# Moving weight splits and the turning of the next rows inside the expert stage of a decoder layer

## The chip, the cores and the metric

The kernel runs on one core of a Trainium2 chip. The metric is the device time of one execution in microseconds (us); lower is better. A core has five engines that run side by side, each through its own instructions in order: TensorE (PE in the profile; its weight loads are PEld), VectorE (DVE), ScalarE (ACT), GpSimd (POOL) and SyncE (SP). They wait for one another by semaphores. Here SyncE issues the plain DMAs and GpSimd the indirect ones, which gather or scatter rows by an index.

## The reference

The layer is a mixer (sliding-window attention beside an mLSTM), a cross attention and a mixture of experts, for 2048 tokens of width 1024, in float32. The change touches only the experts:

```python
def hierarchical_moe(xn, ...):          # 32 experts, top 2 within the best of 4 groups
    ...
    x_pad = zeros.at[dest].set(xt[token_idx[order]])   # tokens sorted by expert, in blocks
    def expert_block(args):
        xb, e = args
        hb = jax.nn.silu(xb @ w_g[e]) * (xb @ w_u[e])  # 1024 -> 512
        return hb @ w_d[e]                             # 512 -> 1024
    y_pad = lax.map(expert_block, ...)
    y = y_pad[dest] * gates[order][:, None]
    out = zeros.at[token_idx[order]].add(y)
```

After that the layer's sum is normalised (`norm_final`). How many tokens an expert has depends on the data: 128 on average, more for some and fewer for others.

## The kernel before

Products are made in float32 precision from two float32r halves, hi and lo: `split` makes hi on ScalarE (a cast) and lo on VectorE (the difference), and three matmuls (hi by hi, hi by lo, lo by hi) give one product (`mm3`, L125 to L127). Weights are split too. One expert has 12 weight pieces of 128 x 1024: four of the gate (w_g), four of up (w_u), four of down (w_d). They are loaded by SyncE into a ring of 9 raw tiles (`we_raw`) and split into a ring of 16 places (`we_hi`, `we_lo`); a raw tile's next load is issued when its split is done (`next_load`). So an expert's 12 pieces and four of the next one's are held at once, and the split of piece 4 of the next expert writes the place of piece 0 (gate) of this one.

The loop over the 32 experts (`phase3`) handles each in these steps, and expert x works ahead for x+1 and x+2:

- the full block A of 128 rows: gate product, SiLU (`full_gate`, run for x+1 at the end of x), up product, product with the gate weight (`times`), turning of the hidden rows by TensorE (`turn_h`), turning of the next expert's A rows (`next_rows(x, 0)`), and the gather of the A rows of x+2 on GpSimd;
- a branch on the count. With more than 128 tokens, `half_within` does a block B of 64 rows: its gate and up products, SiLU, turning of the hidden rows and down product, and a scatter-add of the result to DRAM. Here hi and lo of the 64 rows lie side by side in one operand of 128 columns, so the two halves of the sums come out on different partitions and are added (`both`: a ScalarE copy and a VectorE add). Of the 8 splits that are due, four (`todo[:4]`, up pieces of x+1) are done in this arm: `step(1)` behind SiLU, `step(3)` behind the down product. Without block B, the other arm does these four splits alone. With more than 192 tokens, `later_blocks` handles further blocks L of 64 rows; since the four splits have overwritten the gate pieces, these are first loaded again (`reload`), through the tiles `again` and `yA`;
- the down product of A (`full_down`, `down_turn`), with the other four splits (`todo[4:]`) and, behind its third quarter (k == 2), the turning of the next expert's B rows (`next_rows(x, 1)`: eight transposes, then a cast and a subtraction in `put`) and the gather of the B rows of x+2.

As built, the first two quarters of A's down product (12 matmuls `pu<-..hT`) stand ahead of the branch on TensorE; the order on TensorE, ScalarE and VectorE is as the code is written inside `as_written` (a chain of order-only dependencies). From expert 10 or so on, finished rows are also normalised and given out in between (`norm`): squares on ScalarE, the root on GpSimd, scaling on VectorE.

Tiles: `both` holds the B rows of the next expert in its upper 64 partitions (`xg["B"]`) and block B's hidden rows and results in its lower 64 (`hu`); `xTB` is the turned form of B rows, `xTA` of A rows; `hTB` the turned hidden rows of block B; `pt`, `pu`, `pd`, `pg` are PSUM tiles, three for `pt`; `yA` is the sum of A before its scatter-add. A block L's rows go to `yA` and their turned form to `xTB`.

Of the kernel before, what the change touches and what calls it, by code (L numbers as in the profile page):

```python
# [10 lines left out]
F32R = mybir.dt.float32r  # L11
# [8 lines left out]
P = 128  # L20
# [11 lines left out]
HB = 64  # L32
# [11 lines left out]
def together(*parts):  # L44

    parts = [iter(p) for p in parts]
    while parts:
        parts = [p for p in parts if next(p, p) is not p]


def by(n, part):

    for i, _ in enumerate(part):
        if i % n == n - 1:
            yield
# [11 lines left out]
class Net:  # L67
# [1338 lines left out]
    def phase3(self):  # L1406
        nc, tc, a = self.nc, self.tc, self.a
        with ExitStack() as cx:
            e = lambda **k: cx.enter_context(tc.tile_pool(reuse_waits="tile", **k))
            self.io = e(name="io3", bufs=1)  # L1410
            self.sm = e(name="sm3", bufs=2)
            self.we2 = e(name="we2", bufs=1)
            self.ps_g = e(name="ps_g", bufs=1, space=PSUM)
            self.ps_u = e(name="ps_u", bufs=2, space=PSUM)
            self.ps_t = e(name="ps_t3", bufs=3, space=PSUM)
            self.ps_d = e(name="ps_d", bufs=2, space=PSUM)
            t = lambda name, shape, dt=F32: self.io.tile(shape, dt, name=name)


            both = t("both", [P, D])  # L1420
            self.xg, self.hu = {"A": t("xgA", [P, D], F32R), "B": both[HB:P, :]}, both[:HB, :]
            self.hT = [t(f"hT{i}", [P, 4, P], F32R) for i in range(2)]
            self.xT = {tg: [t(f"xT{tg}{i}", [P, 8, P], F32R) for i in range(n)] for tg, n in (("A", 2), ("B", 1))}

            self.yA = t("yA", [P, D])

            self.again = t("again", [P, D])
            self.xg["L"], self.xT["L"] = self.yA[:HB, :], self.xT["B"]
            for g in self.xg.values():
                nc.vector.memset(g.bitcast(F32), 0.0)  # L1430

            self.flags = t("flags", [1, 2, NEXP], I32)
            for i, n in enumerate((P, P + HB)):
                nc.vector.tensor_scalar(out=self.flags[:, i, :], in0=self.counts[:, :NEXP], scalar1=float(n), scalar2=None,
                                        op0=ALU.is_gt)
            self.infos = [self.expert_info(x) for x in range(3)]
            rows = [self.expert_rows(0, b) for b in range(2)]
            with self.as_written():
                self.weights_ahead(9)
                self.turned_rows(*rows[0])()  # L1440
                self.weights_ahead(10)
                self.turned_rows(*rows[1])()
                self.weights_ahead(12)
                for b in range(2):
                    self.expert_rows(1, b)
                cnt, flags = self.full_gate(0, self.ws)
            self.open_norm()
            for x in range(NEXP):
                ws, self.ws = self.ws[:12], self.ws[12:]
                if x + 3 < NEXP:  # L1450
                    self.infos.append(self.expert_info(x + 3))
                todo = self.next_splits(8)
                last = x + 1 == NEXP
                if last:
                    self.late_norms()
                norm = self.norm_ahead(x)
                with self.as_written():
                    self.full_up(x, ws)
                with tc.If(cnt > P, label=f"more{x}") as more:  # L1459
                    self.hint(f"most{x}", flags)  # L1460
                    self.group_puts = []
                    with self.as_written():
                        ahead = norm() if last else None
                        self.half_within(x, ws, todo[:4], ahead)
                        if last:
                            self.full_down(x, ws, [], ahead)
                    self.later_blocks(x, cnt, ws, todo[:4])
                with more.Else():
                    self.group_puts = []
                    with self.as_written():  # L1470
                        if last:
                            self.full_down(x, ws, [], norm())
                        else:
                            self.splitter(todo[:4])(4)
                if not last:
                    with self.as_written():
                        self.full_down(x, ws, todo[4:], norm())
                        cnt, flags = self.full_gate(x + 1, self.ws)
# [211 lines left out]
    def half_within(self, x, ws, todo, norm):  # L1690

        info, step = self.infos[x][1], self.splitter(todo)
        h, u, hT = self.half_tiles()
        pg = self.pd()
        self.gate(pg, "B", ws)
        pu = [self.half_pu(0)]
        self.up(pu[0], "B", ws, 0)
        self.half_silu(h, pg)
        step(1)
        self.half_times(h, u, pu[0], info, 0)  # L1700
        pu.append(self.half_pu(1))
        self.up(pu[1], "B", ws, 1)
        self.turn_h(h, hT, 0)
        self.half_times(h, u, pu[1], info, 1)
        pd = [self.pd() for _ in range(2)]
        self.down(pd, hT, ws, (0,))
        self.turn_h(h, hT, 1)
        self.down(pd, hT, ws, range(1, 4))
        step(3)
        self.half_out(self.hu, pd, info, "B", norm)  # L1710

    def later_blocks(self, x, cnt, ws, over):
# [25 lines left out]
    def down_turn(self, pd, hT, x, ws, step, norm, late):  # L1738
        for k in range(4):
            self.down(pd, hT, ws, (k,))  # L1740
            step(2 if k == 1 else 1)
            if k == 2:
                self.next_rows(x, 1)()
            self.steps(norm, k == 2, late[k])
        info = self.infos[x][0]
        y = self.sums_of.get("A", self.yA)
        for n in range(2):
            yn = y[:, n * 512:n * 512 + 512]
            if self.sums_of:
                self.nc.vector.tensor_tensor(out=yn, in0=pd[n], in1=yn, op=ALU.add)  # L1750
            else:
                self.nc.scalar.copy(out=yn, in_=pd[n])  # L1752
        if self.sums_of:
            out = [(info, self.yA), *self.due]
            self.due = []
            ssq, r = self.stats(P, len(out))
            self.square(y, ssq, 0)
            self.gain(self.nc.vector, y, self.yA)
            root = self.root_steps(ssq, r)
            next(root)  # L1760
            next(root)
            for at, y in out[1:]:
                self.gain(self.nc.vector, y)
            together(by(2, root), norm)
            for j, (at, y) in enumerate(out):
                rj = r[:y.shape[0], j:j + 1]
                if j:
                    self.nc.scalar.activation(out=y, in_=y, func=AF.Copy, scale=rj)
                else:
                    self.nc.vector.tensor_scalar(out=y, in0=y, scalar1=rj, scalar2=None, op0=ALU.mult)  # L1770
                self.give_apart(at, y)
        else:
            self.add_rows(info, y)
# [265 lines left out]
```

## Time and profile before

| | |
|---|---|
| median of 3 runs | 2336.86 us (2336.54 to 2350.87) |
| the profiled execution | 2337.82 us |
| its span, first to last instruction | 2336.1 us |
| granted TensorE clock over the span | 0.95 |
| TensorE busy | 2091.7 us (90%) |
| VectorE busy | 1558.4 us (67%) |
| ScalarE busy | 1272.3 us (54%) |
| GpSimd busy | 445.1 us (19%) |
| DMA, mean | 186 GB/s |

The busy times are of one profiled execution, from whose own time a sum is to be made. A row's busy share is a mean over stages with different limits; what a step is worth is read in its stage, from what ends a wait last. [...]

### The profile page before, as it was taken

The page shows a single profiled execution, that of the slowest core. Times are in us where ns is not written, and L with a number is a line of the kernel's source. Part 1 is how long each engine was busy: PE and PEld are TensorE (multiplying, and loading weights), DVE is VectorE, ACT ScalarE, POOL GpSimd, SP SyncE. Part 2 cuts the span into 40 slices and gives each one's busy share as a digit, 9 for nine tenths or more (in the row PEclk, how much of TensorE's full clock was granted, in tenths as well). Part 3 has the DMA queues.
Part 4 walks back from the last instruction along what each step waited for, and adds up shares of the span by engine and source line. Part 5 has one row for each costly group of instructions (what it writes and reads, how often), then busy time and mean ns, then how long its engine had stood idle before and what let it go on. Part 6 is the DMA issues. An engine that isn't in the chain of part 4 may idle for free. (4 is left out here: it accounts for less than half of the span.)

```text
span 2336.1 us, 36449 instructions
## 1 busy us (share of the span) xinstructions
PE 2091.7 (90%) x12173; PEld 1790.3 (77%) x12173; DVE 1558.4 (67%) x3586; ACT 1272.3 (54%) x2479; POOL 445.1 (19%) x536
## 2 busy tenths in 40 slices
PE   6999999999999999899985695799999898988985
PEld 5998888988878888898974573677877777777764
DVE  6278876478776756577767453775877768776665
ACT  6267875368763332444542442654766657666553
POOL 1000000000000000133323110111222433523325
PEclk9999999999999999999998797899999999899997
DMA  5533444534578876334555662876988879987743
GB/s 167 127 113 105 116 140 135 133 101 114 145 190 232 231 199 182 118 127 101 114 148 101 188 220 90 269 269 213 315 271 275 282 236 320 314 310 259 248 135 92
DMA packets 266262, 434.75 MB, mean 186 GB/s; under 512 B 53232, under 2 KB 175216, under 8 KB 265952
## 3 DMA queue, kind: packets, MB, share of 16 engines
q1 hardware_dynamic: 245216, 381.25, 52.9%
q0 software_dynamic: 20736, 49.85, 8.1%
q8 instruction: 135, 2.21, 0.4%
q14 instruction: 175, 1.43, 0.2%
HBM read 356.97 MB, written 92.71 MB: 192 GB/s over the span
## 5 line engine op out<-in xcount | busy, mean ns | idle before, releaser
L77 DVE TENSOR_TENSOR we_lo<-we_raw,we_hi 128x1024 fp32r<-128x1024 f32 x384 | 449.1, 1220 | 118.4 <-ACT we_hi L76 111.8
L76 ACT CAST we_hi<-we_raw 128x1024 fp32r<-128x1024 f32 x384 | 380.8, 1054 | 50.6 <-SPq L1459 20.1
L125 PE MATMUL pu<-we_hi,xTA 128*128 128x256 f32 x512 | 148.8, 291 | 25.2 <-ACT yA L1752 25.2
L125 PE MATMUL mm<-hT,w_hi 128*128 128x512 f32 x416 | 166.4, 401 | 0.9 <-ACT hT L327 0.9
L126 PE MATMUL mm<-hT,w_hi 128*128 128x512 f32 x416 | 166.1, 399 | 0.0
L127 PE MATMUL mm<-hT,w_lo 128*128 128x512 f32 x416 | 165.9, 399 | 0.0
L127 PE MATMUL mm<-w_hi,hT 128*128 128x324 f32 (+1 forms) x512 | 152.6, 298 | 0.0
L125 PE MATMUL mm<-w_hi,hT 128*128 128x324 f32 (+1 forms) x512 | 152.6, 298 | 0.0
L126 PE MATMUL mm<-w_lo,hT 128*128 128x324 f32 (+1 forms) x512 | 152.0, 297 | 0.0
L126 PE MATMUL pu<-we_lo,xTA 128*128 128x256 f32 x512 | 148.0, 289 | 0.0
L127 PE MATMUL pu<-we_hi,xTA 128*128 128x256 f32 x512 | 147.7, 288 | 0.0
L125 PE MATMUL pu<-we_hi,hT 128*128 128x512 f32 x256 | 113.0, 441 | 18.6 <-PEq L1459 7.4
L589 POOL TENSOR_TENSOR sq<-sq 128x256 f32<-128x256 f32 x16 | 12.6, 786 | 589.6 <-ACT sq L586 589.6
L125 PEld LDWEIGHTS pu<-we_hi,xTA 128*128 128x128 f32 x512 | 100.5, 196 | 30.1 <-ACT yA L1752 29.1
L126 PE MATMUL pu<-we_lo,hT 128*128 128x512 f32 x256 | 107.1, 418 | 0.0
L127 PE MATMUL pu<-we_hi,hT 128*128 128x512 f32 x256 | 105.1, 411 | 0.0
L125 PE MATMUL pg<-we_hi,xTA 128*128 128x512 f32 x256 | 103.8, 406 | 0.0
L126 PE MATMUL pg<-we_lo,xTA 128*128 128x512 f32 x256 | 103.4, 404 | 0.0
L127 PE MATMUL pg<-we_hi,xTA 128*128 128x512 f32 x256 | 102.5, 400 | 0.0
L126 PEld LDWEIGHTS pu<-we_lo,xTA 128*128 128x128 f32 x512 | 100.4, 196 | 0.9
L127 PEld LDWEIGHTS pu<-we_hi,xTA 128*128 128x128 f32 x512 | 100.5, 196 | 0.0
L125 PEld LDWEIGHTS mm<-w_hi,hT 128*128 128x128 f32 x512 | 96.5, 188 | 1.4 <-ACT o_ev L484 0.8
(501 smaller groups left out, 6067.5 us busy)
## 6 DMA issues: line engine op xcount, KB each, us to landing
we_raw<-in_w_e_gate_dram SPq DMA_DIRECT2D x128, 512.0 KB, 7.3
we_raw<-in_w_e_up_dram SPq DMA_DIRECT2D x128, 512.0 KB, 6.6
we_raw<-in_w_e_down_dram SPq DMA_DIRECT2D x128, 512.0 KB, 9.5
w_raw<-in_w_in_dram SPq DMA_DIRECT2D x56, 256.0 KB, 3.6
q_in<-q_d SPq DMA_DIRECT2D x32, 256.0 KB, 4.3
qk_d<-acc SPq DMA_DIRECT2D x32, 256.0 KB, 3.4
at_d<-at SPq DMA_DIRECT2D x32, 256.0 KB, 2.9
at_in<-at_d SPq DMA_DIRECT2D x32, 256.0 KB, 7.6
```

Of the source, the lines that this page charges most:

```text
L76: first = nc.scalar.copy(out=hi, in_=src)
L77: (low or nc.vector).tensor_tensor(out=lo, in0=src, in1=hi.bitcast(F32), op=ALU.subtract)
L125: first = mm(ps, lhsT=wh, rhs=xh, start=start, stop=False)
L126: mm(ps, lhsT=wh, rhs=xl, start=False, stop=False)
L127: mm(ps, lhsT=wl, rhs=xh, start=False, stop=stop)
L589: nc.gpsimd.tensor_tensor(out=sq[:, 0:2], in0=sq[:, 0:2], in1=sq[:, 2:4], op=ALU.add)
```

## The change

In `half_within`, two of the four splits move ahead of SiLU (`step(2)` right behind the gate product), the other two stay behind the down product (`step(2)` for `step(3)`). The turning of the next B rows, with the gather that follows it, leaves `down_turn` and goes into both arms: in `half_within` its transposes stand behind the turning of B's first hidden half and its cast and subtraction behind those of the second; in the other arm the transposes stand ahead of the four splits and the cast and subtraction behind them. Since `xTB` then already holds the next expert's rows when `later_blocks` runs, a block L's rows get a turned form of their own (`xTL`, 4 KB more in each partition) and are gathered into `hu`.

```diff
@@ phase3
-            self.xg["L"], self.xT["L"] = self.yA[:HB, :], self.xT["B"]
+            self.xg["L"], self.xT["L"] = self.hu, [t("xTL", [P, 8, P], F32R)]
...
                         else:
+                            put = self.next_rows(x, 1)
                             self.splitter(todo[:4])(4)
+                            put()
@@ half_within
         self.gate(pg, "B", ws)
+        step(2)
         pu = [self.half_pu(0)]
         self.up(pu[0], "B", ws, 0)
         self.half_silu(h, pg)
-        step(1)
         self.half_times(h, u, pu[0], info, 0)
         pu.append(self.half_pu(1))
         self.up(pu[1], "B", ws, 1)
         self.turn_h(h, hT, 0)
+        put = self.next_rows(x, 1)
         self.half_times(h, u, pu[1], info, 1)
         pd = [self.pd() for _ in range(2)]
         self.down(pd, hT, ws, (0,))
         self.turn_h(h, hT, 1)
+        put()
         self.down(pd, hT, ws, range(1, 4))
-        step(3)
+        step(2)
         self.half_out(self.hu, pd, info, "B", norm)
@@ down_turn
             step(2 if k == 1 else 1)
-            if k == 2:
-                self.next_rows(x, 1)()
             self.steps(norm, k == 2, late[k])
```

Line numbers in rows of the changed kernel are 3 higher in these functions (L1617 is L1620, L1620 is L1623, L1795 is L1798, L1800 is L1803, L1779 is L1782, L1582 is L1585).

On ScalarE, in the arm with block B, before: behind the branch come the copy of the gate sums and SiLU (L1795, L1800), the first weight cast, the copies of the two up products with the cast of the turned hidden half between them, and three weight casts.

```order
L1459 COMPARE_AND_BRANCH
L1795 COPY both<-pd 64x512
L1800 ACTIVATE both<-both 64x512
L76 CAST we_hi_14564<-we_raw_13928 128x1024
L1795 COPY both<-pd 64x256
L76 CAST hTB<-pt_19921 128x2x64
L1795 COPY both<-pt_19904 64x256
L76 CAST hTB<-pt_19935 128x2x64
L76 CAST we_hi_14569<-we_raw_13930 128x1024
L76 CAST we_hi_14576<-we_raw_8236 128x1024
L76 CAST we_hi_14581<-we_raw_8237 128x1024
```

The same place on ScalarE now.

```order
L1460 COMPARE_AND_BRANCH
L76 CAST we_hi_14565<-we_raw_13928 128x1024
L76 CAST we_hi_14570<-we_raw_13930 128x1024
L1798 COPY both<-pd 64x512
L1803 ACTIVATE both<-both 64x512
L1798 COPY both<-pd 64x256
L76 CAST hTB<-pt_20051 128x2x64
L1798 COPY both<-pt_20034 64x256
L76 CAST hTB<-pt_20077 128x2x64
L76 CAST xTB_14423<-pt_20056 128x8x64
L76 CAST we_hi_14577<-we_raw_8236 128x1024
L76 CAST we_hi_14582<-we_raw_8237 128x1024
```

Two weight casts moved ahead of the first copy, none stands between SiLU and the copy of the up product, and the cast of the next B rows (`xTB`) came in behind the second hidden half.

On TensorE, in the same arm, before: the last up matmul, the first two transposes of the hidden rows (L1779), the first quarter of B's down product, the next two transposes.

```order
L1617 MATMUL pt_19904<-we_hi_9304,xTB_14423 128x256
L1779 MATMUL pt_19921<-ident,both 128x64 x2
L1617 MATMUL pd<-we_hi_14454,hTB 128x512
L1620 MATMUL pd<-we_lo_14455,hTB 64x512
L1617 MATMUL pd<-we_hi_14454,hTB 128x512
L1620 MATMUL pd<-we_lo_14455,hTB 64x512
L1779 MATMUL pt_19935<-ident,both 128x64 x2
```

The same place on TensorE now.

```order
L1620 MATMUL pt_20034<-we_hi_9304,xTB_14423 128x256
L1782 MATMUL pt_20051<-ident,both 128x64 x2
L120 MATMUL pt_20056<-ident,both 128x64 x8
L1620 MATMUL pd<-we_hi_14455,hTB 128x512
L1623 MATMUL pd<-we_lo_14456,hTB 64x512
L1620 MATMUL pd<-we_hi_14455,hTB 128x512
L1623 MATMUL pd<-we_lo_14456,hTB 64x512
L1782 MATMUL pt_20077<-ident,both 128x64 x2
```

The eight transposes of the next B rows (L120, source `both`) came in between the hidden rows' first transposes and the down product.

On TensorE, in A's down product behind the join of the arms, before: the second half of its third quarter, the eight transposes, the start of the last quarter.

```order
L125 MATMUL pu<-we_hi_14464,hT_14419 128x512
L126 MATMUL pu<-we_lo_14465,hT_14419 128x512
L127 MATMUL pu<-we_hi_14464,hT_14420 128x512
L120 MATMUL pt_20272<-ident,both 128x64 x8
L125 MATMUL pu<-we_hi_14469,hT_14419 128x512
```

The end of the arm without block B on TensorE now, the join (L1460) and the start of the third quarter.

```order
L120 MATMUL pt_20369<-ident,both 128x64 x8
L1460 UNCONDITIONAL_BRANCH
L125 MATMUL pu<-we_hi_14465,hT_14419 128x512
L126 MATMUL pu<-we_lo_14466,hT_14419 128x512
L127 MATMUL pu<-we_hi_14465,hT_14420 128x512
```

The transposes moved out of the product to the head of the join; that arm held no TensorE work before.

## Rows read from the trace of the kernel before

**Rows 1.** Busy us (instructions) by stretch, clock, DMA share, GB/s: experts 0, 8; sum.

```profile
1304.60:1342.20 37.60, 33.78 (x185) 27.74 (x185) 23.48 (x31) 21.56 (x31) 5.54 (x4) 0.95 0.65 215
...
1606.70:1642.60 35.90, 32.08 (x186) 26.47 (x184) 21.78 (x29) 19.39 (x30) 6.29 (x5) 1.00 0.65 207
...
sum 520.90, PE 470.22 PEld 382.54 DVE 325.46 ACT 288.09 POOL 120.37; mean PE 33.59 PEld 27.32 DVE 23.25 ACT 20.58 POOL 8.60
```

**Rows 2.** The same view for expert 5, without block B.

```profile
1513.60:1533.80 20.20, 20.05 (x117) 17.17 (x116) 16.87 (x19) 14.69 (x20) 4.55 (x4) 1.00 1.00 351
```

**Rows 3.** Order of time in block B of expert 7: start, us, what, [idle before <-releaser].

```profile
1586.18 0.39 PE L1617 MATMUL pd<-we_hi,xTB 128*128 128x512 f32 x1
...
1590.05 0.58 ACT L1795 COPY both<-pd 64x512 f32<-64x512 f32 x1 [4.87 <-PE pd L1617]
...
1590.67 0.68 DVE L1796 TENSOR_TENSOR both<-pd,both 64x512 f32<-64x512 f32 x1 [4.66 <-ACT both L1795]
...
1591.38 0.63 ACT L1800 ACTIVATE both<-both 64x512 f32<-64x512 f32 x1 [0.75 <-DVE both L1796]
...
1591.60 0.29 PE L1617 MATMUL pd<-we_hi,xTB 128*128 128x256 f32 x1
...
1591.92 1.03 ACT L76 CAST we_hi<-we_raw 128x1024 fp32r<-128x1024 f32 x1
...
1592.86 0.36 ACT L1795 COPY both<-pd 64x256 f32<-64x256 f32 x1
...
1592.98 1.23 DVE L77 TENSOR_TENSOR we_lo<-we_raw,we_hi 128x1024 fp32r<-128x1024 f32 x1 [1.63 <-ACT we_hi L76]
...
1594.13 0.41 DVE L1796 TENSOR_TENSOR both<-pd,both 64x256 f32<-64x256 f32 x1
1594.57 0.48 DVE L1641 SCALAR_TENSOR_TENSOR both<-both,infoA 64x256 f32<-64x256 f32 x1
...
1595.20 0.31 PE L1779 MATMUL pt<-ident,both 64*128 64x64 f32 x2 [1.45 <-DVE both L1641]
...
1596.18 0.50 PE L1617 MATMUL pd<-we_hi,hTB 128*128 128x512 f32 x1 [0.68 <-DVE hTB L77]
```

**Rows 4.** TensorE's waits in the expert stage: waiter, releaser: us, times, longest.

```profile
PE pt L1779 <- DVE both L1641: 21.7, 15, 1.5
PE pt L120 <- DMA yA<-xn_d,infoB: 21.2, 1, 21.2
PE pd L1617 <- DVE hTB L77: 12.3, 17, 1.4
...
PE pt L120 <- DVEq L1714: 7.0, 6, 1.3
```

**Rows 5.** Order of time on TensorE in A's down product of expert 28.

```profile
2200.13 1.14 PE L120 MATMUL pt<-ident,both 64*128 64x64 f32 x8 [1.29 <-DVEq L1714]
```

**Rows 6.** Busy us by stretch, as rows 1, inside expert 7.

```profile
1597.25:1600.66 3.41, 3.41 (x10) 2.32 (x10) 1.87 (x3) 2.82 (x4) 0.00 (x0) 0.50 0.03 7
```

**Rows 7.** SyncE's queue in order of time, ahead of expert 7's block B.

```profile
1573.35 1.48 SPq L1513 DMA_DIRECT2D we_raw<-in_w_e_up_dram  x3
```

**Rows 8.** DMA issues of the page: count, KB each, us to landing.

```profile
we_raw<-in_w_e_up_dram SPq DMA_DIRECT2D x128, 512.0 KB, 6.6
```

**Rows 9.** Order of time on ScalarE, the copies of expert 22's sums.

```profile
2022.10 1.07 ACT L1752 COPY yA<-pu 128x512 f32<-128x512 f32 x2 [3.66 <-DMA out_dram<-y_fin,list]
```

**Rows 10.** Order of time in expert 2, from the last reload to block L's gate.

```profile
1430.47 1.23 DVE L77 TENSOR_TENSOR we_lo<-yA,we_hi 128x1024 fp32r<-128x1024 f32 x1 [1.62 <-ACT we_hi L76]
1431.97 0.96 POOL L1582 DMA_INDIRECT yA<-xn_d,infoB  x1 [14.96 <-DVE we_lo L77]
...
1434.98 1.19 PE L120 MATMUL pt<-ident,yA 64*128 64x64 f32 x8 [21.23 <-DMA yA<-xn_d,infoB]
...
1444.36 0.58 ACT L1795 COPY both<-pd 64x512 f32<-64x512 f32 x1 [7.56 <-PE pd L1617]
```

**Rows 11.** TensorE's branches at the arms: count, ns min/median/max, first and last start.

```profile
L1459 PEldq COMPARE_BRANCH  x32: 70/218/6019, 1318.4 to 2289.8; - x32
```

## The prediction

> **What bounds the kernel now.** I read the granted clock and busy times by stretch first, then the order of time inside one expert, then who waited for whom. The change touches the expert stage alone, which runs from 1304.6 us to the end at 2336.1 us. Call the expert at place x of the loop "expert x". The 16 experts with more than 128 tokens also run a 64-row block B; 14 of them (all but 2 and 31) take 520.9 us, 37.2 us each, with TensorE marked busy for 33.6 us and a clock of 0.95 in most [rows 1]. An expert without block B takes 20.2 us of which TensorE is busy 20.05, at clock 1.00 [rows 2]. So where there is no block B, TensorE is the limit and has no hole; where there is one, the block costs 17 us, and the holes must lie in it.
>
> The order of time in expert 7 shows them [rows 3]. TensorE starts B's gate product at 1586.18. ScalarE, idle for 4.87 us, copies the upper half of the gate sums at 1590.05; VectorE adds (0.68), ScalarE does SiLU (0.63, ended at 1592.0). Then the queue order bites: ScalarE next casts a weight tile (1.03), so the copy of the first up product starts only at 1592.86 although that product was done at 1591.9; and VectorE's 1.23 us subtraction for the same split sits ahead of the add (1594.13) and the product with the gate weight (1594.57). TensorE, through with the second up product at 1593.75, gets its input at 1595.17: a hole of 1.45 us. A second hole, 0.68 us, follows, since the down product needs both halves of the turned tile just made. The chain of waits has these as 21.7 us in 15 and 12.3 us in 17 places [rows 4]. A third one: the eight transposes of the next B rows inside the full block's down product wait 1.29 us in expert 28 for VectorE's last work of the arm [rows 5], 7.0 us in 6 places altogether [rows 4]. And after such holes the clock halves: 0.50 for 3.41 us in expert 7 [rows 6].
>
> **The change part by part.** All sums are against the profiled execution, 2337.82 us (span 2336.1 and 1.7 around it); the median of the runs shown is 1.0 us below that.
>
> *Two splits ahead of SiLU.* Nothing is added: 2 casts and 2 subtractions move from behind SiLU into ScalarE's 4.87 us of idle time. They write the ring places of the gate weights that block B is just reading, so the first must wait until B's gate has used its first piece, which is 4 of 16 matmuls at 0.23 us, 1.1 us after its start (1586.18 becomes zero). Casts: 1.1 to 2.1 and 2.1 to 3.1. Subtractions: 2.1 to 3.4 and 3.4 to 4.6. The copy of the gate sums comes at 3.9 as before and ends at 4.45; the add can start at 4.6 instead of 4.5 and ends at 5.3; SiLU ends at 5.9; the copy of the first up product ends at 6.3, its add at 6.7, the product at 7.2. TensorE ends the second up product at 7.6. The hole of 1.45 us closes with 0.4 us to spare: 14 times 1.42 is 19.9 us. The cover is the gate product's 3.8 us; without it each split would push SiLU by 1.2 us. The weight tiles to be split are there: the later of the two loads was issued at 1573.35, 12.8 us ahead, and a load of this kind lands after 6.6 us in the median [rows 7, 8]; among the 16 block-B experts that lead is 11 us at the shortest. SyncE then issues the two refilling loads up to 8 us earlier, which costs nothing and helps.
>
> *The next 64 rows turned inside the arm.* The eight transposes (1.14 us in [rows 5]) leave the full block's down product and stand behind the first transposes of B's own hidden tile. There they fill the 0.68 us hole and the rest is the time they took anyway: 14 times 0.68 is 9.5 us. With them out of the down product, the 7.0 us of waits for the end of VectorE's arm go. The cast (0.59) and subtraction (0.68) of the turned rows stand behind those of B's second hidden half, before the two remaining splits, where only the arm's closing copies follow. In the other arm (16 experts) the same eight transposes come 1.4 us earlier on TensorE, and cast and subtraction come before four splits instead of after: TensorE's count is unchanged, and those splits feed the next expert's down product, some 15 us on. I cost it at nothing; it would cost up to 1.3 us an expert if ScalarE and VectorE had no slack there. On GpSimd the gather of the rows after next is issued in the arm, ahead of the scatter-add of B, whose data is ready only at the arm's end. In the other arm it comes ahead of the queue's pass through the join, for which ScalarE's copies of the sums (yA) wait where GpSimd runs late, as at 2022.10 [rows 9]; one gather more in that path, and one less since the A gather now precedes the root steps: between -0.7 and +0.7 us in 6 experts, taken as 0, bounds 4 us either way.
>
> *The clock.* The 14 experts lose (1 - clock) x length, worked out over the 14 rows and summed, 22.0 us. Expert 8 has the same first two holes and 1.00 [rows 1], so holes do not always cost it; an expert without holes has 1.00 [rows 2]. If 1.42, 0.68 and 1.29 go, what is left is 0.4 us at the arm's end. I take 20.0 of the 22.0 as won; the bounds are 0 and 22.0.
>
> *Rows of the late block.* One expert (2) has more than 192 tokens. Its third block gathered its rows into yA, which is also a reload tile, so the gather waited for the last reload's subtraction: 1430.47 plus 1.23, gather at 1431.97, transposes at 1434.98 and a gate product that ended at 1444.33 [rows 10], after 21.2 us without work for TensorE [rows 4]. With a tile of its own the rows are turned while the four reloads run, and the gate ends one piece (4 matmuls, at half clock 1.7 us) after the last subtraction at 1431.7, near 1433.5: 10.8 us less. TensorE stays at half clock a little longer, up to 1.7 us; I take 9, bounds 7 and 12. Expert 2's block B wins 4 us like the others.
>
> Sum: 19.9 + 9.5 + 7.0 + 20.0 + 9 + 4 = 69.4 us; 2337.8 - 69.4 = 2268.4. Expert 31 has no weights left to split and no next rows: nothing. **Forecast: 2268 us.** What is next late in the arm is VectorE, which ends its last add some 3 us after TensorE's last B matmul; nothing of TensorE waits for that once the transposes are gone.
>
> **Rivals.** *The clock is not won back.* The holes shrink but the arm's end still has 0.4 us and a branch; with 0 of 22.0 the time is about 2290. For it: some holes fell without a halving and others with it, so the link isn't one to one. Against it: the holeless experts at 1.00.
>
> *The splits are held to the end of the gate product* (so the change does not do what it says). If the release of the weights' places comes only with the gate's last matmul, both casts start at 3.9, the second subtraction ends at 7.3, add 8.0, SiLU 8.6, copy 9.0, product 9.95, where today it ends at 8.9: the first hole grows by 1.0 us, 14 us in all, no clock is won, 9.5, 7.0 and 9 stay: 2337.8 - 11.5, near 2326, no change. Against it: ScalarE's copy at 1590.05 was released in the middle of TensorE's stream, by one matmul of it [rows 3]. [...]
>
> *Branch fetch, the slower side.* Of TensorE's 32 branches at the start of the arms one took 6.02 us, with a median of 0.22 [rows 11]. The arm without block B held no TensorE work and now does, and the way from one arm to the join gets longer. If 16 entries and 16 exits each took half of that longest one, 3.0 us, that is 96 us against 69: 2364. It decides from 23 more such holds on. Against it: the added code is eight transposes and a jump an expert, and half of the branches took 0.22 us or less. [...]
>
> **How the numbers follow.** Forecast 0.72; clock not won 0.13 (2290); splits held 0.07 (2326); branch fetch 0.03 (2364); more than I count, below 2252, 0.05. The range takes in the first two with their bounds: all of the clock, 12 for the late block and 4 from GpSimd give about 2259 and some more for shorter stalls elsewhere 2252; no clock, 7 for the late block and 4 lost to GpSimd give 2296, with a few us for the spread of runs 2300. The measurement tells about 1% (the runs shown spread by 0.6%): faster by over 1% is below 2313.5, so faster 0.90, same 0.07, slower 0.03.
>
> **What would show it.** In the profile after: ScalarE's two casts inside B's gate product and none between SiLU and the next copy; TensorE's wait before B's first transposes gone from the list of waits, or down to a few tenths; no wait at the transposes of the next rows in either arm; the 14 block-B experts at 32 to 34 us with clock 1.00; the late gather issued before the reloads end. The forecast is wrong if the casts start after the gate's last matmul, if the half clock stays in these experts, if TensorE in the other arm waits for rows not yet gathered, or if experts without block B grow beyond 20.2.

## The result and the profile after

The changed kernel takes 2265.45 us in the median of 6 runs (2258.9 to 2277.3), the kernel before 2341.16 in 6 (2336.5 to 2350.9): a ratio of 0.969, interval 0.967 to 0.971. The profiled executions are 2258.90 against 2337.82 us, 78.9 less, with spans of 2257.2 and 2336.1.

First the expert stage by stretches (us from and to, length, busy us of each engine with its count of instructions, granted clock, DMA share, GB/s): the first of the 14 experts with block B, expert 7, and the sum of the 14.

```profile
1301.00:1334.40 33.40, 32.96 (x185) 27.48 (x185) 21.43 (x30) 19.54 (x28) 3.61 (x4) 0.96 0.72 254
...
1540.20:1572.20 32.00, 31.56 (x186) 26.32 (x185) 22.00 (x29) 18.95 (x29) 5.12 (x5) 1.00 0.71 234
...
sum 471.20, PE 447.67 PEld 372.03 DVE 326.07 ACT 285.06 POOL 131.02; mean PE 31.98 PEld 26.57 DVE 23.29 ACT 20.36 POOL 9.36
```

The 14 took 520.9 us before [rows 1] and take 471.2, 49.7 less. Expert 7 takes 32.0 us at a clock of 1.00. It took 36.1 at 0.95 in the profile before:

```profile
1570.60:1606.70 36.10, 33.53 (x186) 27.33 (x185) 21.88 (x29) 18.27 (x28) 5.46 (x5) 0.95 0.66 208
```

The records of the granted clock, a share of full speed, read 1.00 or 0.50 in both profiles and nothing between, so 0.95 is a mean over time at each. In expert 7 before, TensorE's 128x512 matmuls started 0.43 us apart inside the stretch at 0.50 [rows 6] and 0.23 behind it, so that four took 1.7 us at half clock, as the prediction has it for the late block:

```profile
1599.07 0.63 PE L1617 MATMUL pd<-we_hi,hTB 128*128 128x512 f32 x1
1599.50 0.63 PE L1620 MATMUL pd<-we_lo,hTB 128*64 128x512 f32 x1
1599.92 0.63 PE L1617 MATMUL pd<-we_hi,hTB 128*128 128x512 f32 x1
...
1600.73 0.39 PE L1617 MATMUL pd<-we_hi,hTB 128*128 128x512 f32 x1
1600.96 0.40 PE L1620 MATMUL pd<-we_lo,hTB 128*64 128x512 f32 x1
1601.19 0.39 PE L1617 MATMUL pd<-we_hi,hTB 128*128 128x512 f32 x1
```

In the same view expert 5, without block B, and the sum of the 16 without block B, after the change:

```profile
1488.50:1508.30 19.80, 19.80 (x118) 17.29 (x117) 17.36 (x20) 15.11 (x22) 4.54 (x3) 1.00 1.04 367
...
sum 357.70, PE 326.99 PEld 284.93 DVE 285.22 ACT 249.18 POOL 144.17; mean PE 20.44 PEld 17.81 DVE 17.83 ACT 15.57 POOL 9.01
```

Expert 5 had 20.2 us [rows 2]. The sum of the 16 in the profile before:

```profile
sum 372.80, PE 336.26 PEld 286.44 DVE 293.23 ACT 251.37 POOL 132.62; mean PE 21.02 PEld 17.90 DVE 18.33 ACT 15.71 POOL 8.29
```

So the 16 lost 15.1. Expert 2 (with the late block) went from 79.4 to 68.2, expert 31 from 58.4 to 59.0, and the stage began 3.5 us earlier. 49.7 + 15.1 + 11.2 - 0.6 + 3.5 is 78.9: the whole difference.

TensorE's waits in the expert stage (waiter, releaser: us, times, longest), against [rows 4]:

```profile
PE pu L125 <- ACT yA L1755: 32.9, 7, 11.8
PE pt L120 <- DMA both<-xn_d,infoB: 17.0, 1, 17.0
PE pt L1782 <- DVE hA L1644: 8.5, 8, 3.2
PE pu L126 <- PEq L1719: 5.2, 8, 2.1
PE pt L120 <- DVE we_lo L77: 3.1, 2, 1.8
PE pd L1620 <- DVE hTB L77: 2.0, 2, 1.4
```

The group of 21.7 us at B's first transposes is gone, that of 12.3 us at B's down product is down to 2.0 in experts 2 and 31, and the 7.0 us for the end of VectorE's arm are gone. At the top, as before the change, stands the wait for yA, now 32.9 us. Waits for TensorE's own branch at the start of the arms (L1459), 7.4 us before, are no longer in the list. The two lines before:

```profile
PE pu L125 <- ACT yA L1752: 25.2, 7, 11.0
PE pu L125 <- PEq L1459: 7.4, 4, 3.0
```

Block B of expert 7 in order of time on ScalarE, VectorE and TensorE (start, us, what, [idle before <- releaser]), to be read against [rows 3]; the gate product starts at 1555.84.

```profile
1556.97 2.00 ACT L76 CAST we_hi<-we_raw 128x1024 fp32r<-128x1024 f32 x2 [2.14 <-PE pd L1620]
1559.73 0.58 ACT L1798 COPY both<-pd 64x512 f32<-64x512 f32 x1 [0.76 <-PE pd L1620]
1561.07 0.64 ACT L1803 ACTIVATE both<-both 64x512 f32<-64x512 f32 x1 [0.75 <-DVE both L1799]
1561.61 0.36 ACT L1798 COPY both<-pd 64x256 f32<-64x256 f32 x1
...
1558.05 2.36 DVE L77 TENSOR_TENSOR we_lo<-we_raw,we_hi 128x1024 fp32r<-128x1024 f32 x2 [2.40 <-ACT we_hi L76]
1560.35 0.68 DVE L1799 TENSOR_TENSOR both<-pd,both 64x512 f32<-64x512 f32 x1
...
1562.46 0.48 DVE L1644 SCALAR_TENSOR_TENSOR both<-both,infoA 64x256 f32<-64x256 f32 x1
...
1563.15 0.27 PE L1620 MATMUL pt<-we_hi,xTB 128*128 128x256 f32 x1
1563.36 0.27 PE L1782 MATMUL pt<-ident,both 64*128 64x64 f32 x1
...
1563.54 1.00 PE L120 MATMUL pt<-ident,both 64*128 64x64 f32 x7
1564.46 0.50 PE L1620 MATMUL pd<-we_hi,hTB 128*128 128x512 f32 x1
```

Both casts lie inside the gate product, released by its matmuls, the first 1.13 us after its start. SiLU starts 5.23 us after that start. The product with the gate weight is done at 1562.94, 0.4 us before TensorE's transposes of the hidden rows start (1563.36), and no bracket, so no wait, stands at them. The eight transposes of the next rows (seven in the row of 1.00 us) reach to the down product, which has no bracket either.

### The profile page after: what moved, and what is told of

It reads as the page before. It is cut to its first block, busy times and chain, and to the rows that moved or that the text cites. A ratio compares the mean times of both kernels' runs of the same rounds, so it can differ in the third digit from the quotient of the medians.

```text
span 2257.2 us, 36582 instructions
## 1 busy us (share of the span) xinstructions
PE 2055.1 (91%) x12173; PEld 1776.2 (79%) x12173; DVE 1555.3 (69%) x3586; ACT 1271.4 (56%) x2479; POOL 466.6 (21%) x536
## 5 line engine op out<-in xcount | busy, mean ns | idle before, releaser
L125 PE MATMUL pu<-we_hi,xTA 128*128 128x256 f32 x512 | 149.7, 292 | 32.9 <-ACT yA L1755 32.9
L125 PE MATMUL pu<-we_hi,hT 128*128 128x512 f32 x256 | 106.0, 414 | 5.4 <-ACT both L1798 2.2
L127 PE MATMUL pu<-we_hi,hT 128*128 128x512 f32 x256 | 103.2, 403 | 0.0
L1788 POOL DMA_INDIRECT y_d<-yA,infoA x31 | 71.9, 2320 | 126.0 <-ACT yA L1755 64.6
```

The lines of the kernel that those rows point to most:

```text
L125: first = mm(ps, lhsT=wh, rhs=xh, start=start, stop=False)
L127: mm(ps, lhsT=wl, rhs=xh, start=False, stop=stop)
L1788: self.nc.gpsimd.indirect_dma_start(out=self.y_d[:, :], out_offset=bass.IndirectOffsetOnAxis(ap=info[:, 0:1], axis=0), in_=y, in_offset=No ...
```

## The experiments

Ratios are to runs of the kernel before on the same chip.

**One part alone.** The splits alone, on the kernel before:

```diff
         self.gate(pg, "B", ws)
+        step(2)
...
         self.half_silu(h, pg)
-        step(1)
...
-        step(3)
+        step(2)
         self.half_out(self.hu, pd, info, "B", norm)
```

> The kernel before with the two splits moved ahead of SiLU alone; the next B rows are still turned in the full block's down product, and the late block is as before. Both theories: the hole of 1.42 us ahead of the first transposes of B's hidden rows goes in the 14 block-B experts (-19.9 us). Theory A, the clock follows the longest hole: what is left (0.68 us, and 1.29 us in six experts) is too short to bring the half clock back, so most of the 20 us of clock comes with the splits: near 2301 us. Theory B, the clock needs all the holes gone: the 14 experts stay near 0.95, and the time is near 2321 us. The list of waits keeps about 9.5 us at B's down product either way.

Measured: 2292.87 us (2291.4 to 2299.1), ratio 0.980 (0.976 to 0.984). Expert 7, the sum of the 14, and one line of TensorE's waits:

```profile
1556.70:1590.00 33.30, 32.04 (x186) 26.40 (x185) 21.84 (x29) 19.01 (x29) 5.41 (x5) 1.00 0.69 228
...
sum 480.10, PE 454.47 PEld 373.55 DVE 326.47 ACT 287.60 POOL 122.79; mean PE 32.46 PEld 26.68 DVE 23.32 ACT 20.54 POOL 8.77
```

```profile
PE pd L1617 <- DVE hTB L77: 11.6, 16, 1.4
```

Theory A holds, and by more than it said. The 14 experts take 480.1 us, 40.8 less than before: 20.2 for the 14 holes of 1.42 to 1.46 us, and (1 - clock) x length falls from 22.0 to 4.7 us, though the hole of 0.68 us is still there. In these experts most of the half clock goes with the hole of 1.42 us and not with that of 0.68. It is no strict link: expert 8 had both holes and 1.00 before [rows 1].

The turning alone, on the changed kernel with the splits put back:

```diff
         self.gate(pg, "B", ws)
-        step(2)
...
         self.half_silu(h, pg)
+        step(1)
...
-        step(2)
+        step(3)
         self.half_out(self.hu, pd, info, "B", norm)
```

> The changed kernel with the splits put back behind SiLU and the down product, so only the turning of the next rows (both arms) and the late block's tiles differ from the kernel before. Own working: -9.5 (hole of 0.68 us filled), -7.0 (transposes no longer wait for the end of VectorE's arm), about -4.6 for the late block, and about -6 in the experts without block B, whose join of arms no longer stands bare (0.4 us each in the profile after). The hole of 1.42 us stays. Theory A, the clock follows the longest hole: the half clock stays, near 2314 us. Theory B, the clock goes with the sum of holes: part of the 20 us comes, near 2300 us. A rival from the queue: the eight transposes now stand in front of the wait for VectorE's product, so the hole is filled with them only partly and nothing is won: 2325 us.

Measured: 2304.32 us (2299.5 to 2309.4), ratio 0.983 (0.980 to 0.987). Expert 7, the sum of the 16 experts without block B, and TensorE's wait that stays:

```profile
1557.20:1592.20 35.00, 33.16 (x186) 27.14 (x185) 21.24 (x28) 18.78 (x29) 4.38 (x5) 0.95 0.63 203
```

```profile
sum 360.70, PE 326.08 PEld 283.03 DVE 290.62 ACT 253.38 POOL 153.95; mean PE 20.38 PEld 17.69 DVE 18.16 ACT 15.84 POOL 9.62
```

```profile
PE pt L1782 <- issue: 19.6, 14, 1.4
```

The clock did as theory A says: the hole of 1.4 us stays in 14 experts, and the clock loses 32.9 us in them (22.0 before). The median is 10 us below theory A's 2314; the profiled execution (2309.4) is the slowest of the four and lies 28.4 us below the one before, about the 27 that theory A adds up, but by other terms. The 14 experts give only 8.6 us, since the clock loses 10.9 more; expert 2 gives 10.7; and the 16 experts without block B take 360.7 us, 12.1 less than before and twice what the expectation had. In the run with the splits alone they take 372.0. So these experts get shorter with the turning, which the prediction had at nothing.

**More and fewer splits ahead.** `step(3)` behind the gate and `step(1)` at the end:

```diff
         self.gate(pg, "B", ws)
-        step(2)
+        step(3)
...
-        step(2)
+        step(1)
         self.half_out(self.hu, pd, info, "B", norm)
```

> The changed kernel with three splits ahead of SiLU and one behind the down product. Theory, slack of 0.4 us: the third cast must wait for the gate's third piece, about 3.05 us after the gate's start, and ends at 4.1, so the copy of the gate sums ends at 4.7 and not 4.45; the third subtraction (1.22 us) stands ahead of the add, which starts at 5.8 and not 4.6; SiLU ends at 7.1, the product at 8.4, while TensorE is done with the second up product at 7.6: a hole of 0.8 to 1.0 us comes back in 14 experts, 11 to 14 us, less up to 4 us that the shorter end of the arm gives, and up to 20 us of clock: between 2273 and 2297 us. Rival, idle time is free wherever it lies: 2265 us, with the 0.44 us hole at the arm's end gone, even 2260 us.

Measured: 2270.32 us (2266.8 to 2281.7), ratio 0.971 (0.967 to 0.975). VectorE in expert 7 (gate product from 1557.4), and the expert's row:

```profile
1559.65 3.50 DVE L77 TENSOR_TENSOR we_lo<-we_raw,we_hi 128x1024 fp32r<-128x1024 f32 x3 [2.39 <-ACT we_hi L76]
1563.06 0.68 DVE L1799 TENSOR_TENSOR both<-pd,both 64x512 f32<-64x512 f32 x1
```

```profile
1541.80:1574.60 32.80, 31.66 (x186) 26.35 (x185) 22.09 (x29) 18.95 (x29) 5.34 (x4) 1.00 0.70 229
```

The third subtraction holds the add, and the hole comes back, 0.67 us instead of 0.8 to 1.0: 0.8 us in an expert. The clock stays at 1.00 with it, so the upper half of the expectation falls, and the time lies 3 us below its lower end. Its interval overlaps that of the changed kernel; the row shows the loss, the total doesn't.

`step(1)` behind the gate and `step(3)` at the end:

```diff
         self.gate(pg, "B", ws)
-        step(2)
+        step(1)
...
-        step(2)
+        step(3)
         self.half_out(self.hu, pd, info, "B", norm)
```

> The changed kernel with one split ahead of SiLU and three behind the down product. Theory, ScalarE's queue order at the arm's end: SiLU is as early as with two splits, but the copy of B's first sum, for which TensorE's next quarter of A's down product waits 0.44 us in the profile after, now stands behind one more cast (1.05 us): the hole at the arm's end grows to about 1.45 us, 14 us in 14 experts, and if a hole of that size brings the half clock, as the one of 1.42 us did before, up to 20 us more: between 2279 and 2299 us. Rival, only the way to SiLU counts: one split more at the end is hidden, 2265 us.

Measured: 2276.89 us (2272.1 to 2286.1), ratio 0.974 (0.970 to 0.977). The theory falls: the hole at the arm's end stays 0.43 to 0.44 us in nearly every block-B expert, and the 14 experts take 471.6 us in sum, as with two. What grows is TensorE's wait in a full block, for VectorE's product:

```profile
PE pt L1782 <- DVE hA L1644: 12.8, 19, 2.1
```

That is 19 waits and 12.8 us for 8 and 8.5. The block-B experts 1, 7, 17 and 29 take 32.4 to 32.5 us for 32.0, each with such a wait of 0.21 to 0.28 us that the changed kernel does not have: there the splits left over push what follows. More of the growth, 2.8 us, falls in experts without block B, whose arm this run leaves as it was, and is not shown to come from the splits.

**The arm's end.** The late tile of below and the third split between the second up product and the down product:

```diff
         self.half_times(h, u, pu[1], info, 1)
+        step(1)
         pd = [self.pd() for _ in range(2)]
...
-        step(2)
+        step(1)
         self.half_out(self.hu, pd, info, "B", norm)
```

> The run with the late tile for experts 0 to 8, and besides the third split moved from behind B's down product to ScalarE's idle 1.57 us between the copy of the second up product and the cast of the second hidden half. Theory, the arm's end: the copy of B's first sum then waits for TensorE's last matmul alone and no more for a cast, so the hole at the arm's end falls from 0.44 to 0.2 us; the subtraction delays the turned half by 0.4 us, which the second quarter covers. 3 us in 14 experts: near 2250 us. Rival, the delayed turned half is late: a hole of 0.1 to 0.4 us comes in at B's third quarter and eats it, 2253 to 2256 us.

Measured: 2268.94 us (2261.9 to 2278.3), ratio 0.969 (0.967 to 0.972): no win over the run with the late tile alone, 2260.81 on the same chip. The copy of B's first sum on ScalarE and TensorE's next matmul behind the arm, expert 7:

```profile
1565.49 1.07 ACT L1800 COPY both<-pd 64x512 f32<-64x512 f32 x2 [0.81 <-ACT we_hi L76]
...
1565.47 0.40 PE L1620 MATMUL pd<-we_hi,hTB 128*128 128x512 f32 x1
1566.31 0.50 PE L125 MATMUL pu<-we_hi,hT 128*128 128x512 f32 x1 [0.43 <-ACT both L1800]
```

ScalarE's two copies start at 1565.49 and take 1.07 us, the first is done at 1566.07; TensorE goes on at 1566.31 all the same, 0.43 us after its own last matmul. The releaser named in the bracket is only the last event that the profile knows; TensorE's branch out of the arm (at 1566.06, 0.19 us) lies in this hole. The run with one split ahead settles it, at the same place in its expert 7:

```profile
1577.18 0.51 PE L125 MATMUL pu<-we_hi,hT 128*128 128x512 f32 x1 [0.43 <-PEq L1719]
...
1577.49 0.58 ACT L1798 COPY both<-pd 64x512 f32<-64x512 f32 x1
```

There the copy of B's first sum starts only after TensorE has gone on, and the hole is the same, put down to TensorE's own branch. It is no wait for ScalarE, and neither of the two moves of a split closed it: 0.43 us in both runs.

The turning at the arm's end:

```diff
-        put = self.next_rows(x, 1)
         self.half_times(h, u, pu[1], info, 1)
...
-        put()
         self.down(pd, hT, ws, range(1, 4))
+        put = self.next_rows(x, 1)
         step(2)
         self.half_out(self.hu, pd, info, "B", norm)
+        put()
```

> The changed kernel with the turning of the next rows in the arm with block B moved to its end: the transposes behind B's last matmul, cast and subtraction behind the closing copies and adds; the other arm is as changed. Theory, the transposes are worth the hole that they fill: the hole of 0.68 us ahead of B's down product comes back in 14 experts (+9.5 us), and the transposes (1.1 us) fill the one of 0.44 us at the arm's end (-6.2 us): near 2269 us, the clock as after, since 0.68 us left it at 1.00 in the run with three splits ahead. Rival, as before the change the end of VectorE's arm is waited for again (the turned rows' cast and subtraction stand last in the arm, and the join holds what comes behind): 2275 to 2285 us.

Measured: 2273.38 us (2272.1 to 2280.1), ratio 0.971 (0.968 to 0.974). The hole of 0.68 us is back in TensorE's waits:

```profile
PE pd L1620 <- DVE hTB L77: 12.3, 17, 1.4
```

A block-B expert without other waits takes 33.0 us for 32.0, and the hole of 0.44 us is still there behind the transposes: the branch's again. The clock stays 1.00. The theory's place was right and its sum short: of the 1.0 us, 0.68 is the hole, 0.3 is busy time of TensorE (31.88 us in expert 7 for 31.56), and the 0.44 us that the transposes were to fill did not come back.

**The late block.** In the profile after, in order of time on GpSimd, TensorE and ScalarE:

```profile
1397.72 1.47 POOL L1788 DMA_INDIRECT y_d<-both,infoA  x1 [5.74 <-DVE both L1799]
1406.77 0.97 POOL L1585 DMA_INDIRECT both<-xn_d,infoB  x1 [7.59 <-issue]
...
1412.04 1.19 PE L120 MATMUL pt<-ident,both 64*128 64x64 f32 x8 [17.01 <-DMA both<-xn_d,infoB]
...
1413.26 0.59 ACT L76 CAST xTL<-pt 128x512 fp32r<-128x512 f32 x1 [6.51 <-PE pt L120]
1413.74 1.05 ACT L76 CAST we_hi<-again 128x1024 fp32r<-128x1024 f32 x1
...
1421.08 0.58 ACT L1798 COPY both<-pd 64x512 f32<-64x512 f32 x1 [5.34 <-PE pd L1620]
```

The rows go to the lower half of `both`, from which block B's scatter-add is just read: the gather is issued 9.05 us after the scatter, 7.59 of them idle on GpSimd (the scatter's end is recorded at 1406.04). ScalarE's cast of the turned rows then waits 6.51 us, and two of the four reload casts stand right behind it in its queue. The next run keeps the rows in yA as before and reloads through a tile that is idle at expert 2:

```diff
-            self.xg["L"], self.xT["L"] = self.hu, [t("xTL", [P, 8, P], F32R)]
+            self.xg["L"], self.xT["L"] = self.yA[:HB, :], [t("xTL", [P, 8, P], F32R)]
...
-        t = (self.again, self.yA)[i % 2]
+        t = (self.again, self.nt[1])[i % 2]
```

> The changed kernel with the late block's rows gathered to yA, as before the change, and the reloads done through `again` and one of the tiles of the final norm (idle at expert 2), so that neither tile waits for the other. Theory, two tiles hold the late block now: its gather waits 8.4 us for block B's scatter to leave the lower half of `both`, and after it A's copies of the sums to yA wait for the second reload, 11.8 us in expert 3. Then the gather is issued 9 us earlier, the gate ends about 2 us after the last reload's subtraction and not 3.9, and the wait in expert 3 falls to some 5 us, bounded by the loads: 8 to 10 us less, near 2256 us. Rival, the loads alone set both: the gate ends no earlier, and expert 3 waits as long for the up pieces as it did for yA: 2265 us.

Measured: 2282.07 us (2274.7 to 2293.2), ratio 0.975 (0.972 to 0.979), slower than the changed kernel. The late block itself, on GpSimd, TensorE and ScalarE:

```profile
1398.78 0.96 POOL L1585 DMA_INDIRECT yA<-xn_d,infoB  x1 [0.30 <-issue]
...
1405.27 1.22 PE L120 MATMUL pt<-ident,yA 64*128 64x64 f32 x8 [10.94 <-DMA yA<-xn_d,infoB]
...
1414.15 0.58 ACT L1798 COPY both<-pd 64x512 f32<-64x512 f32 x1 [2.49 <-PE pd L1620]
```

Here the theory holds: from B's last matmul to the copy of the late gate it is 30.6 us before, 26.1 after the change and 19.8 now; expert 2 is 6.2 us shorter and expert 3 6.4. From expert 11 on 34 us are lost, most of them in a wait that neither theory had:

```profile
PE pg L125 <- ACT pg L1945: 23.2, 6, 5.8
```

The tile belongs to the final norm. Its squares (L1945) use `pg` as their output, and ScalarE stood idle ahead of them until SyncE had passed the end of the arm (15.5 us in 3 places), since the arm now reloads through that tile. To try this reading, the tile is used for experts 0 to 8 alone:

```diff
-        t = (self.again, self.nt[1])[i % 2]
+        t = (self.again, self.nt[1] if x < COME[0][0] else self.yA)[i % 2]
...
+            self.xg["L"] = self.yA[:HB, :] if x + 1 < COME[0][0] else self.hu
             first = self.infos[x][2], self.expert_rows(x, 2)
```

> The changed kernel with the other reload tile of the run before for experts 0 to 8 only (x + 1 below the first expert that normalises rows), where that tile of the norm is idle; from there on as in the changed kernel. Theory, in that run the norm steps waited for SyncE's pass through the arm because they share the tile, and that alone cost what experts 11 to 29 lost; the late block's own win, 6.2 us in expert 2 and 6.4 in expert 3, stays: near 2253 us, with experts 10 to 30 as in the profile after. Rival, what is won early is given back by DMA and GpSimd behind expert 10, whatever the tile: 2265 us or more.

Measured: 2260.81 us (2255.0 to 2268.1), ratio 0.966 (0.963 to 0.968). The waits at `pg` are gone, which bears the reading out. Experts 2 and 3 keep 10.3 us of their win; experts 22 to 24 give 5.3 us of it back, and against the changed kernel the intervals overlap. In the two profiles the expert stage itself is 6.5 us shorter, but it began 11.7 us later (1312.8), after stages that neither kernel changes.

**The gather.** In the runs with the turning moved (the first late tile aside), experts 19, 22, 23 and 28 wait for yA 3.5 to 7 us each. The gather alone goes back:

```diff
-        if x + 2 < NEXP:
-            self.expert_rows(x + 2, b)
+        if b == 0 and x + 2 < NEXP:
+            self.expert_rows(x + 2, 0)
...
             step(2 if k == 1 else 1)
+            if k == 2 and x + 2 < NEXP:
+                self.expert_rows(x + 2, 1)
```

with the changed kernel itself beside it on the same chip:

> The changed kernel itself, for its runs beside the two others on one chip and for a second profile. What is the change's own should stand in both profiles: 31.9 to 32.0 us for a block-B expert without waits, 19.6 to 19.8 us for one without block B, the waits for yA in experts 19, 22, 23 and 28. What is chance should differ: the start of the expert stage (1300 to 1313 us in the runs so far), single experts from 11 on. Near 2265 us.

> The changed kernel with the gather of the B rows of x+2 put back behind the third quarter of A's down product; the turning itself stays in both arms. Theory, GpSimd's order: with the gather in the arm, ahead of the join, experts 19, 22, 23 and 28 wait 3.5 to 5.4 us for yA in every run with the turning moved (19 to 22 us in all, expert 3 left out), while the two kernels with the gather at its old place wait 14 to 17 us in smaller pieces; so the waits fall back to 14 to 17 us and the time to about 2259 us. Rival, the DMA queues set these waits and the experts before them are only shorter now: the waits stay at 19 to 22 us, 2265 us.

Measured: 2262.54 us (2254.1 to 2268.6), ratio 0.965 (0.962 to 0.967) for the changed kernel, and 2253.57 (2247.3 to 2256.8), 0.960 (0.958 to 0.963) with the gather back. The second profile of the changed kernel repeats what is its own (expert 7 32.0, expert 5 19.7, yA 33.3 us) and differs at the stage's start (1303.8) and by up to 1.6 us in single experts (2, 11, 13, 16). With the gather back TensorE's wait for yA is

```profile
PE pu L125 <- ACT yA L1757: 32.7, 6, 11.8
```

The theory falls: the waits for yA stay. The kernel seems 9 us faster nonetheless, with intervals that just touch; in the two profiles, 5.0 us of span apart, the wait for `hA` at the full block's transposes is 4.3 us for 8.9. How the gather's place reaches that wait was not tried further.

> The run with the late tile for experts 0 to 8 and the gather put back as well, as the candidate for a version that beats the changed kernel. If both theories hold, their wins add up: -10 us in experts 2 and 3 and -5 us in the waits for yA, near 2250 us; if only the late tile counts, near 2256 us, and if the waits for yA grow by what the start of the stage gains, 2261 us as in the run with the late tile.

Measured: 2252.53 us (2248.8 to 2257.9), ratio 0.961 (0.958 to 0.963). It and the one before are the fastest of the study; the late tile adds nothing to the median that these runs can tell, though experts 2 and 3 are 10.3 us shorter in its profile: experts 15, 19, 22, 23 and 24 are 8.8 us longer than with the gather back alone, and experts 13 and 16 6.9 shorter.

## Why the prediction was right, and what in it was off

The forecast of 2268 us was right, and so was its main mechanism. Its sum of 69.4 us stands against 78.9 between the two profiles, with terms that missed on both sides. That it came so close is partly luck: the experts without block B gave 15.1 us that it had at nothing, and made up for terms that fell short.

- *Splits ahead of SiLU, 19.9.* Right to a few tenths (20.2 us of holes went in the 14 experts): the first cast at 1.13 us (worked out: 1.1), SiLU's end at 5.87 (5.9), the product's at 7.1 (7.2), 0.4 us to spare, the wait of 21.7 us (15 places) gone. The rival that the splits are held to the gate's end fell: the casts were released by matmuls in its middle. That two is the number is shown from both sides: three cost 0.8 us in an undisturbed expert, one costs 0.4.
- *The next rows turned in the arm, 9.5 and 7.0.* Both waits went from the list. The runs with the turning alone and with the turning at the arm's end show that the transposes are worth the hole that they fill.
- *The clock, 20.0 of 22.0.* 16.2 came (22.0 to 5.8 us in the 14 experts; ten of them have 1.00). Against the rival, all of it comes with the splits alone (22.0 to 4.7). What is left falls in experts 0, 11, 13 and 28; the last three have other holes of 2 to 5 us, at yA, at `hA` and at a branch.
- *The late block, 9 with bounds 7 and 12.* Off: 4.6 us, 30.6 to 26.1 (24.7 in the second profile of the changed kernel). The step that failed is that the rows "are turned while the four reloads run": the new place of the rows is itself in use, by block B's scatter. With that wait away, in the run that also reloads through another tile, 10.8 us are won, which is what the prediction had worked out before it allowed for the clock; the run with that tile for experts 0 to 8 wins 9.9. [rows 10] showed such a wait on yA; that the new tile has a reader in flight too was to be had from GpSimd's queue, where B's scatter-add stands ahead of the gather.
- *The other arm at nothing.* The large miss, 15.1 us, in favour of the change. It comes with the turning: 12.1 us in the run with the turning alone, 0.8 with the splits alone. A part is seen in every such expert without other waits: 19.65 to 19.8 us instead of 20.0 to 20.2. Before, the arm was empty on TensorE, so its jump in and its jump out followed each other with no matmul between; in expert 5 the gap between the starts of the last matmul ahead and the first behind was 0.55 us where 0.23 is the pace. Now the eight transposes lie there, and no longer break up A's down product. No run changes the other arm alone, so this reading is argued. By the two profiles, the half clock costs TensorE's busy time in the 16 experts 6.3 us less (17.6 to 11.3), TensorE is idle 5.8 us less, and 3.0 us, 0.2 an expert, is left for its work at full clock. So most of the 15.1 is clock and waits, and part of that is branches.
- *The branches, the rival on the slower side (2364 us).* The opposite came. Of TensorE's branches at the arms' starts and ends, 9 took over 1 us before (32.1 us in sum, the longest 6.02 [rows 11]), and 4 after (13.8 us):

```profile
L1460 PEldq COMPARE_BRANCH  x33: 70/184/4739, 1315.1 to 2229.2; - x33
```

The long branches cost less than they took: before, those at the arms' starts were 6 of the 9 and took 24.3 us, and TensorE waited 7.4 us in 4 places for branches there; after, for none there. Expert 27, which held the branch of 6.02 us, went from 28.0 to 19.7 us, and its clock from 0.80 to 1.00. With the splits alone 8 remain (33.0 us), with the turning alone 4 (14.8), and the second profile of the changed kernel has 5 (14.7): it goes with the turning. The four runs with the late tile have 7 each, the other runs with the turning 4 or 5, so the count also moves with the rest of the code, and what decides it stays open. Each of the 9 and of the 4 ended 1.36 to 1.55 us after the end of a packet of 16 KB on the queue q8, which the pages list as instruction (135 packets and 2.21 MB in the whole run before); these packets had taken 0.9 to 1.3 us. That a long branch waits for its packet is the author's reading of these times; no run tried it.
- *GpSimd and yA, 0 with bounds of 4.* 25.2 to 32.9 us: outside. The gather's place is not the cause, as putting it back showed; experts ahead of these places are shorter now, and why the same four then wait was not settled.
- *Chance.* 3.5 us come from the stages ahead, which the change doesn't touch; the expert stage began between 1300.1 and 1313 us in the profiles of this study.

Set together: the 14 block-B experts gave 49.7 us for 56.4. They were short by 3.8 of clock and by 9.7 of other waits that grew, 5.0 of them at yA (5.4 in expert 28 alone) and 5.4 at `hA`, where these experts had none; against that, 0.3 more came from the first hole, and TensorE's work at full clock is 6.5 shorter, which the prediction did not have. Expert 2 gave 11.2 for 13; the experts without block B gave 15.1 where the forecast had nothing.

## What to carry to other kernels

Before work is put into a producer queue's idle time, work out whether its last piece ends before the item behind it is ready. Here that was so for two splits of four; a third cost 0.8 us in an undisturbed expert, and the arithmetic from a few rows gave the times of the two to a tenth. When a tile is moved off one that is busy, read the queue of everything that still uses the new one, reads by DMA included: here the gather into the new one was issued 9.05 us after the scatter that read it. An arm that was empty for TensorE was not free here: in expert 5 before, 0.55 us lay between the starts of the matmuls on both sides of it where 0.23 is the pace, and work that had to be done anyway could stand there.

## What was not expected of the hardware

- Where a hole of 1.4 us stood in block B, most experts lost clock (0.95 for expert 7 with the turning alone; experts 1 and 11 kept 1.00 there). With one of 0.67 or 0.68 us and no other over 0.5, experts 1, 7, 17 and 29 kept 1.00, with three splits ahead as with the splits alone.
- TensorE's branch out of the arm with block B leaves 0.43 to 0.44 us between matmuls, whether ScalarE's copy comes before or after; where the copy comes first, the profile names ScalarE's event there.
- Each of TensorE's branches over 1 us at the arms ended 1.36 to 1.55 us after the end of a 16 KB packet on q8, the queue listed as instruction: 9 before and 4 after the change.
- The late block's gather, into the rows of `both` that block B's scatter was reading, was issued 9.05 us after that scatter, 7.59 of them idle on GpSimd.
